# A two-layer hybrid backbone: four schedule numbers that hand out input products differently

## The chip, the cores and the metric

The kernel runs as one program on 1 core of one Trainium2 chip. The metric is device microseconds of that core. Three runs of the kernel before took 4359.16, 4373.27 and 4374.07 us; their median is 4373.27 us.

The engines are named as the profile names them: PE is TensorE's matmul, PEld its weight load, DVE is VectorE, ACT is ScalarE, POOL is GpSimd and SP is SyncE, which starts most DMAs here.

## The reference, cut to what matters

There are two layers over a trunk of 256 context tokens and 512 latent tokens. Layer 0 carries all 768 tokens, layer 1 only needs the 512 latent ones at its end. All tensors are fp32.

```python
def token_mixer(hc, hl, cos, sin, w_in, rw, cv, at, w_branch, w_out, ctx_out):
    zc = hc @ w_in                     # one input projection, 1024 -> 10112 columns
    zl = hl @ w_in
    ...
    o_rw_c, o_rw_l = rwkv_branch(rwc, rwl, *rw, ctx_out)      # bidirectional RWKV-7, 16 heads of 64
    o_at_c, o_at_l = attention_branch(atc, atl, *at, cos, sin, ctx_out)  # 8 q heads, 2 kv heads of 128
    o_cv_l = conv_branch(cvl, *cv)     # GLU, depthwise conv 31, LayerNorm, swish
    out_l = merge_branches(o_rw_l, o_cv_l, o_at_l, gtl, w_branch, w_out)
...
def merge_branches(o_rw, o_cv, o_at, z_gate, w_branch, w_out):
    branches = jnp.stack([o_rw, o_cv, o_at], axis=-2)
    proj = jnp.einsum('blnc,ncd->blnd', branches, w_branch)   # three 1024 x 1024 products
    gates = jax.nn.sigmoid(z_gate.reshape(proj.shape))
    return jnp.sum(gates * proj, axis=-2) @ w_out
```

After the mixer comes a norm, a residual and a squared-ReLU MLP (1024 -> 4096 -> 1024), again with norms.

## The kernel before, in words

**Products.** Each fp32 product is made of three fp32r products: `split` (L326) writes a high part on ACT and the rest on DVE or POOL, for the weights (`wh`, `wl`) and for the activations (`hh`, `hl`), and PE adds hi·hi, hi·lo and lo·hi. Products that are to be mixed into other work go into a queue: `job` (L392) appends 8 steps, one for each 128 rows of the weight, and `fill(n)` (L397) takes the next n steps off the queue and writes their matmuls (L412) into the program at that place. One step is called a *fill* here. In layer 0 it is six matmuls of 128x384 (768 tokens), in layer 1 three of 128x512. A fill whose step is 0 or 4 also asks for weights, two to four halves ahead: a DMA on SP (L372), the high part on ACT (L328) and the low part on DVE (L332).

**Spills.** The 36 column blocks of the input projection for attention and the gates (q 0 to 7, k and v 8 to 11, gates 12 to 35) are not used until after the RWKV part. `spill` (L1075) queues such a block, 8 fills, and its end (`spill_done`, L1081) copies the sum to a stage buffer on ACT and sends it to the DRAM tensor `z`.

**The pairs.** `rwkv_phase` (L1139) goes through 16 RWKV heads in 8 pairs. A pair has a merge and batch of small matmuls on PE, a serial chain between PE, DVE and ACT, and the readout; beside it runs the preparation of the next pair, ended by the solve. These are generators that yield estimated microseconds; `weave` (L1059) goes round them and calls `fill` for each estimated microsecond, in a ratio from `SCHED`. So the fills stand between the dependent steps of a pair. The queue also holds the pair's own input products and conv columns. Spills are queued at three places:

```python
            spills(F['early'])                                   # before pair 0
                cum = lambda p: round((32 - F['rest']) * p / 7)
                    spills(cum(p + 1) - cum(p))                  # in each of the pairs 0 to 6
                    spills(len(todo))                            # in the last pair: all that is left
```

After each solve, `s.fill(F['solve'])` takes up to 26 (layer 0) or 34 (layer 1) further fills of the queue. `rw_merge`'s first matmuls (L901) are kept behind the last fill.

**The load stage of attention.** What the last pair has not taken off the queue goes to `att_prep` (L556), which issues the loads of k, the rope table, q and v from `z` on SP (L481, L565) and prepares k and V. It calls `fill(len(s.jobs) // 3)` after each of two k heads and `fill(len(s.jobs) // 2)` after each of two v heads. `merge_phase` (L1250) then takes all that is left, closes the pool of `hh` and `hl`, opens the pool of `oh` and `ol` (9 buffers each) at its place, and makes the operands of branch 0 from the RWKV result (`of` loaded at L1273, `oh` on ACT, `ol` on POOL, both in `split`).

**The heads.** `att_head` (L594) runs 8 query heads, in layer 0 in two segments each (context and latent), in layer 1 in one. After each of its 128-query blocks it takes one fill, and at the end of each segment `pad` fills; these are products of branch 0, 64 fills in all.

**The conv norm.** After the heads, `merge_phase` steps through the LayerNorm of the conv branch with `for _ in range(ln): next(ln); s.fill(3)`: a product with `om` (L491), eight squares on ACT (L497) that POOL adds up in `csum` (L499), and the sum over channels (L502). Then it takes the remaining branch-0 fills and makes the operands of branch 2 from the attention result.

The framework's scheduler puts the instructions of each engine in an order of its own where the dependences allow it, by the program order and estimated costs.

Of the kernel before, what the change touches and what calls it, by code (L numbers as in the profile page):

```python
# [44 lines left out]

SCHED = [dict(open=1.3, first=0.55, mid=0.5, end=0.4, solve=26, early=4, tap0=1, tap1=1, merge=1.2, sums=0, grams=0, rest=9, ln=9, pad=1, last=1.15, tap2=1),
         dict(open=1.2, first=0.4, mid=0.4, end=0.4, solve=34, early=5, tap0=0.8, tap1=0.8, merge=1.4, sums=0, grams=0, rest=9, ln=9, pad=1, last=0.85, tap2=1.1)]


def shape_constants():
# [24 lines left out]
class Kern:  # L77
# [1061 lines left out]
    def rwkv_phase(s, l, P, T):  # L1139
# [3 lines left out]
        with ExitStack() as rc:  # L1143
# [18 lines left out]
            lat = T != TOK  # L1162
            F = s.sched = SCHED[l]
            s.tdebt, s.tratio = 0.0, F['tap0']
# [294 lines left out]
```

## Time and profile before

| | |
|---|---|
| median of 3 runs | 4373.27 us (4359.16 to 4374.07) |
| profiled execution | 4372.14 us |
| its span (first to last instruction) | 4370.4 us |
| mean granted TensorE clock | 0.963 |
| layer 0: merge of pair 1 to end of the last pair's chain | 367.9 to 1317.6 us |
| layer 0: load stage, heads, conv norm | 1317.6 to 1360.0, to 1574.2, to about 1596 us |
| layer 1: merge of pair 1 to end of the last pair's chain | 2611.9 to about 3570 us |
| layer 1: load stage, heads | to about 3607, to about 3782 us |

The stage borders are the starts of the first merge matmul of a pair (L901), of the rope product of k (L521), of the product with `om` (L491), and the end of the last step of the chain. The granted clock is given as a share of 2.4 GHz; 0.5 is 1.2 GHz.

### The profile page before, as it was taken

What the parts mean: (1) busy time and instruction counts of PE and PEld (TensorE: products, weight loads), DVE (VectorE), ACT (ScalarE), POOL (GpSimd) and SP (SyncE); (2) the same over time, 40 slices, a digit from 0 to 9 for tenths busy, and PEclk for the clock granted to TensorE, in tenths of its full rate; (3) what the DMA queues carried; (4) which work ended last, traced back from release to release, by engine and by line L of the source; (5) the groups of instructions that cost most, each with busy time, mean ns of one, the idle gap of its engine ahead of it and who ended that gap; (6) DMA issues with size and microseconds to landing.
All of it is one profiled execution on the core that took longest, in us unless ns stands there. A gap on an engine that the chain in (4) does not pass through costs nothing.

```text
span 4370.4 us, 77114 instructions
## 1 busy us (share of the span) xinstructions
PE 4141.8 (95%) x31232; PEld 3410.5 (78%) x31232; DVE 2723.4 (62%) x5238; ACT 1834.4 (42%) x3586; POOL 287.1 (7%) x349
## 2 busy tenths in 40 slices
PE   6999999999998989899999899999999989898998
PEld 4888888888886679689999677887777765575886
DVE  3788888888855554332323577888888855554344
ACT  3444445444534442332223445555545534433332
POOL 0000000000001022200000100000000000121001
PEclk9999999999999999899999889999999979998998
DMA  4212211112134234343322221112221232242332
GB/s 165 78 47 63 64 53 60 51 55 63 59 100 163 69 120 160 110 152 126 102 86 63 72 70 51 58 59 60 66 62 57 73 119 74 65 140 61 97 94 80
DMA packets 443595, 367.73 MB, mean 84 GB/s; under 512 B 19662, under 2 KB 391528, under 8 KB 437096
## 3 DMA queue, kind: packets, MB, share of 16 engines
q1 hardware_dynamic: 422504, 283.10, 21.6%
q10 hardware_dynamic: 20736, 79.70, 5.0%
q8 instruction: 247, 4.05, 0.4%
q14 instruction: 108, 0.88, 0.1%
HBM read 301.38 MB, written 53.48 MB: 81 GB/s over the span
## 4 chain that ended last, share of the span: by engine, by line
PE 80%; DVE 9%; ACT 5%; issue 2%; DMA 2%; POOL 2%; SPq 0%; ACTq 0%; DVEq 0%; POOLq 0%
PE mm L412 31%; PE mm L389 20%; PE g L815 3%; PE g L633 2%; PE g L939 2%; PE sp L960 2%; PE g L928 2%; PE S L612 2%; PE sp L964 1%; PE yp L978 1%; PE yp L976 1%; PE g L850 1%; PE g L1044 1%; PE g L824 1%; PE g L234 1%
## 5 line engine op out<-in xcount | busy, mean ns | idle before, releaser
L328 ACT ACTIVATE wh<-raw 128x512 fp32r<-128x512 f32 x700 | 441.4, 631 | 1249.8 <-PE mm L389 565.5
L332 DVE TENSOR_TENSOR wl<-raw,wh 128x512 fp32r<-128x512 f32 x700 | 502.0, 718 | 697.6 <-ACT wh L328 685.3
L412 PE MATMUL mm<-hh,wh 128*128 128x384 f32 (+1 forms) x2072 | 647.5, 371 | 15.3 <-ACT hh L328 4.8
L412 PE MATMUL mm<-hl,wh 128*128 128x384 f32 (+1 forms) x2072 | 637.9, 367 | 6.1 <-POOL hl L330 6.1
L412 PE MATMUL mm<-hh,wl 128*128 128x384 f32 (+1 forms) x2072 | 634.8, 365 | 0.0
L471 DVE SCALAR_TENSOR_TENSOR cv<-u,dw,cv 128x783 f32<-128x783 f32 (+1 forms) x480 | 426.7, 889 | 2.8
L412 PEld LDWEIGHTS mm<-hh,wh 128*128 128x128 f32 x2072 | 377.6, 192 | 55.1 <-ACT hh L328 7.3
L412 PEld LDWEIGHTS mm<-hl,wh 128*128 128x128 f32 x2072 | 382.6, 192 | 38.0 <-POOL hl L330 8.8
L412 PEld LDWEIGHTS mm<-hh,wl 128*128 128x128 f32 x2072 | 383.0, 192 | 30.5 <-issue 3.2
L412 PE MATMUL mm<-oh,wh 128*128 128x384 f32 (+1 forms) x768 | 252.9, 384 | 9.5 <-DVE acc L1285 6.0
L412 PE MATMUL mm<-ol,wh 128*128 128x384 f32 (+1 forms) x768 | 239.9, 365 | 10.2 <-POOL ol L330 10.2
L389 PE MATMUL mm<-hh,wh 128*128 128x384 f32 (+1 forms) x768 | 239.5, 367 | 5.3 <-ACT hh L347 3.6
L389 PE MATMUL mm<-hl,wh 128*128 128x384 f32 (+1 forms) x768 | 238.3, 365 | 5.1 <-POOL hl L330 4.6
L412 PE MATMUL mm<-oh,wl 128*128 128x384 f32 (+1 forms) x768 | 238.8, 364 | 0.0
L389 PE MATMUL mm<-hh,wl 128*128 128x384 f32 (+1 forms) x768 | 235.8, 362 | 0.0
L389 PE MATMUL mm<-fh,wh 128*128 128x384 f32 (+1 forms) x768 | 229.9, 353 | 0.0
L389 PE MATMUL mm<-fh,wl 128*128 128x384 f32 (+1 forms) x768 | 229.9, 353 | 0.0
L389 PE MATMUL mm<-fl,wh 128*128 128x384 f32 (+1 forms) x768 | 229.5, 352 | 0.0
L815 PEld LDWEIGHTS g<-KR,BK 64*128 64x128 f32 x1536 | 157.3, 204 | 43.0 <-issue 33.7
L815 PE MATMUL g<-KR,BK 64*128 64x128 f32 (+1 forms) x1536 | 178.3, 306 | 5.2 <-DVE KR L808 3.1
L412 PEld LDWEIGHTS mm<-oh,wh 128*128 128x128 f32 x768 | 139.6, 189 | 51.2 <-ACT wh L328 13.6
L966 ACT ACTIVATE S<-sp,lam 128x64 f32<-128x64 f32 x352 | 92.9, 310 | 206.3 <-PE sp L964 199.4
(297 smaller groups left out, 7239.0 us busy)
## 6 DMA issues: line engine op xcount, KB each, us to landing
raw<-in_w_in_dram SPq DMA_DIRECT2D x316, 256.0 KB
raw<-in_w_ff_dram SPq DMA_DIRECT2D x256, 256.0 KB
wmod<-in_w_mod_dram ACTq DMA_DIRECT2D x48, 1024.0 KB
raw<-in_w_branch_dram SPq DMA_DIRECT2D x96, 256.0 KB
z<-f ACTq DMA_DIRECT2D x40, 384.0 KB
gt<-z SPq DMA_DIRECT2D x24, 384.0 KB
raw<-in_w_out_dram SPq DMA_DIRECT2D x32, 256.0 KB
z<-f ACTq DMA_DIRECT2D x32, 256.0 KB
```

Source lines behind the costliest of these rows:

```text
L328: s.last_hi = nc.scalar.activation(out=hi, in_=src, func=AF.Copy)
L332: nc.vector.tensor_tensor(out=lo, in0=src, in1=hi.bitcast(F32), op=ALU.subtract)
L389: nc.tensor.matmul(ps[:, b, :t1 - t0], lhsT=w[:, k % 4, :], rhs=a[:, t0:t1], start=k == 0 and f == 0, stop=k == KT - 1 and f == 2)
L412: s.last_mm = nc.tensor.matmul(s.jps[:, b, :t1 - t0], lhsT=w[:, k % 4, :], rhs=a[:, t0:t1], start=k == 0 and f == 0, stop=k == KT - 1 and ...
L471: s.tap_pin(nc.vector.scalar_tensor_tensor(out=hold['c'], in0=u[:, k:k + L], scalar=w(k), in1=hold['c'], op0=ALU.mult, op1=ALU.add))
L612: nc.tensor.matmul(sps[:, b, :384], lhsT=lq, rhs=kT[kv][:, 384 * b:384 * b + 384], start=True, stop=True)
L633: nc.tensor.matmul(op[:, :nq], lhsT=V[:, kk, kv * 128:kv * 128 + 128], rhs=PT[:, kk, :nq], start=kk == 0, stop=kk == nk // 128 - 1)
L815: nc.tensor.matmul(gp[h][:, q, 0:n, :], lhsT=BK[ROWS[h], 4 * g + q].rearrange("p a b -> p (a b)"), rhs=KR[ROWS[h], 0:n, 4 * g + q, :], sta ...
L928: nc.tensor.matmul(wu[ROWS[h], q - q0], lhsT=TT[ROWS[h], q, :], rhs=KM[ROWS[h], q].rearrange("p a b -> p (a b)"), start=True, stop=True)
L939: nc.tensor.matmul(ap[ROWS[h], q - q0, 0:n, :], lhsT=W[ROWS[h], q, :], rhs=GB[ROWS[h], h, q, 0:n, :], start=True, stop=True)
L960: nc.tensor.matmul(sp[ROWS[h], d], lhsT=GB[d][:, h, q[d], 0, :], rhs=UV[d][:, h * 12 + q[d], :], start=d == 0, stop=d == 1 and k == 0)
L966: nc.scalar.activation(out=Sn[:, d], in_=sp[:, d], func=AF.Copy, scale=Q['lam', d][:, q[d]:q[d] + 1])
```

## The change: four numbers of the schedule tables

Two lines change, one for each layer. In layer 0 `rest` goes from 9 to 13 and `pad` from 1 to 0. In layer 1 `early` goes from 5 to 7 and `rest` from 9 to 14.

```diff
-SCHED = [dict(open=1.3, first=0.55, mid=0.5, end=0.4, solve=26, early=4, tap0=1, tap1=1, merge=1.2, sums=0, grams=0, rest=9, ln=9, pad=1, last=1.15, tap2=1),
-         dict(open=1.2, first=0.4, mid=0.4, end=0.4, solve=34, early=5, tap0=0.8, tap1=0.8, merge=1.4, sums=0, grams=0, rest=9, ln=9, pad=1, last=0.85, tap2=1.1)]
+SCHED = [dict(open=1.3, first=0.55, mid=0.5, end=0.4, solve=26, early=4, tap0=1, tap1=1, merge=1.2, sums=0, grams=0, rest=13, ln=9, pad=0, last=1.15, tap2=1),
+         dict(open=1.2, first=0.4, mid=0.4, end=0.4, solve=34, early=7, tap0=0.8, tap1=0.8, merge=1.4, sums=0, grams=0, rest=14, ln=9, pad=1, last=0.85, tap2=1.1)]
```

The number of all fills is the same. Where they are taken off the queue, counted in the program that the schedule writes (fills, before and after):

| place | layer 0 | layer 1 |
|---|---|---|
| weave of pair 0 | same | 21, 36 |
| weaves and solves of later pairs | 32 fewer | 39 fewer |
| weave of the last pair | 65, 65 | same |
| `att_prep`, after the k heads and v heads | 7, 39 | 17, 41 |
| each of the 8 heads | 8, 6 | same |
| conv norm, its first 9 steps | 0, 16 | 24, 24 |

The scheduler's order on PE follows this only roughly. Fill matmuls between the first merges of consecutive pairs, on PE, before and after (M1 is the first merge of pair 1):

| layer 0 | before | after | layer 1 | before | after |
|---|---|---|---|---|---|
| M1 to M2 | 432 | 425 | M0 to M1 | 264 | 381 |
| M2 to M3 | 384 | 402 | M1 to M2 | 360 | 317 |
| M3 to M4 | 393 | 385 | M2 to M3 | 254 | 267 |
| M4 to M5 | 453 | 384 | M3 to M4 | 295 | 259 |
| M5 to M6 | 354 | 372 | M4 to M5 | 256 | 235 |
| M6 to M7 | 438 | 355 | M5 to M6 | 264 | 223 |
| M7 to end of chain | 198 | 137 | M6 to M7 | 215 | 192 |
| end of chain to rope of k | 84 | 101 | end of chain to rope of k | 30 | 61 |
| rope of k to `om` | 419 | 497 | rope of k to `om` | 165 | 194 |
| `om` to L502 | 58 | 62 | before M0 | 24 fewer | |
| after L502 | 93 more | | | | |

PE's order in layer 0 around the rope product of k (`kraw`), where the load stage ends and head 0 begins (`vz` is raw v, `kT` the finished k, `qraw` a query head, L628 its transposes), before:

```order
L412 MATMUL mm<-hh,wh 128x384 x2
L412 MATMUL mm<-hl,wh 128x384 x2
L412 MATMUL mm<-hh,wl 128x384 x2
L521 MATMUL g<-kraw,rope 128x512 x2
L589 MATMUL g<-cst,vz 128x128 x4
L608 MATMUL S<-kT_13871,qraw 128x256
L589 MATMUL g<-cst,vz 128x128 x2
L608 MATMUL S<-kT_13871,qraw 128x256
L589 MATMUL g<-cst,vz 128x128 x6
L521 MATMUL g<-qraw,rope 128x512
L628 MATMUL g<-cst,Pm 128x128 x2
L612 MATMUL S<-kT_13871,qraw 128x384
```

The same place in the changed program:

```order
L412 MATMUL mm<-hh,wl 128x384
L521 MATMUL g<-kraw,rope 128x512
L412 MATMUL mm<-hh,wl 128x384
L412 MATMUL mm<-hh,wh 128x384 x2
L412 MATMUL mm<-hl,wh 128x384 x2
L412 MATMUL mm<-hh,wl 128x384 x2
L412 MATMUL mm<-hh,wh 128x384 x2
L412 MATMUL mm<-hl,wh 128x384 x2
L412 MATMUL mm<-hh,wl 128x384 x2
L412 MATMUL mm<-hh,wh 128x384 x2
L412 MATMUL mm<-hl,wh 128x384 x2
L412 MATMUL mm<-hh,wl 128x384 x2
```

Input products now stand between the two rope products of k; further blocks of them stand between the v transposes and the first query products. Before, none stood behind the first rope product.

SP's queue in layer 0 ahead of the loads of k and behind them (`bv` and `orw` belong to the last pair's readout, `raw` is a weight half), before:

```order
L475 DMA ocv<-cv 128x512
L372 DMA raw<-in_w_in_dram 128x4x128 x6
L372 DMA raw<-in_w_branch_dram 128x4x128 x2
L1005 DMA bv<-bv_d_89 128x768
L372 DMA raw<-in_w_branch_dram 128x4x128
L1027 DMA orw<-y 128x768
L372 DMA raw<-in_w_branch_dram 128x4x128
L481 DMA kraw<-z 128x768 x2
L565 DMA rope<-in_rope_dram 128x1152
L481 DMA qs<-z 128x768
L481 DMA vz<-z 128x768 x2
```

And in the changed program:

```order
L475 DMA ocv<-cv 128x512
L372 DMA raw<-in_w_in_dram 128x4x128 x6
L1005 DMA bv<-bv_d_89 128x768
L372 DMA raw<-in_w_in_dram 128x4x128
L1027 DMA orw<-y 128x768
L372 DMA raw<-in_w_in_dram 128x4x128
L481 DMA kraw<-z 128x768 x2
L565 DMA rope<-in_rope_dram 128x1152
L481 DMA qs<-z 128x768
L481 DMA vz<-z 128x768 x2
L481 DMA qs<-z 128x768 x7
L372 DMA raw<-in_w_in_dram 128x4x128 x2
```

Two weight halves fewer stand ahead of `kraw`, and the weights that follow the loads are those of input products.

POOL's queue in layer 0 from the heads to the conv norm (`ol<-of` up to L228 is branch 0 and the start of branch 2, later ones branch 2, `cvx` is branch 1), before:

```order
L330 TENSOR_TENSOR ol<-of,oh 128x768 x15
L228 MEMSET sc_16402 128x256
L229 COPY sc_16402<-sc 128x8x2
L499 TENSOR_TENSOR csum<-csum,csq 128x768
L330 TENSOR_TENSOR ol<-of,oh 128x768
L499 TENSOR_TENSOR csum<-csum,csq 128x768 x6
L330 TENSOR_TENSOR ol<-cvx,oh 128x768 x8
```

And in the changed program:

```order
L330 TENSOR_TENSOR ol<-of,oh 128x768 x9
L228 MEMSET sc_16402 128x256
L229 COPY sc_16402<-sc 128x8x2
L499 TENSOR_TENSOR csum<-csum,csq 128x768 x2
L330 TENSOR_TENSOR ol<-of,oh 128x768
L499 TENSOR_TENSOR csum<-csum,csq 128x768
L330 TENSOR_TENSOR ol<-of,oh 128x768
L499 TENSOR_TENSOR csum<-csum,csq 128x768 x4
L330 TENSOR_TENSOR ol<-of,oh 128x768 x5
L330 TENSOR_TENSOR ol<-cvx,oh 128x768 x8
```

Seven of branch 2's eight low parts now stand among the sums of the conv norm or behind them; before, seven of the eight stood ahead of them.

## Rows read from the trace of the kernel before

**Rows 1.** The page, part 1: busy time of each engine.

```profile
PE 4141.8 (95%) x31232; PEld 3410.5 (78%) x31232; DVE 2723.4 (62%) x5238; ACT 1834.4 (42%) x3586; POOL 287.1 (7%) x349
```

**Rows 2.** Windows: stretch, its us, busy us of each engine, clock, DMA share, GB/s.

```profile
1900.00:2400.00 500.00, 500.00 (x2902) 477.81 (x2900) 151.84 (x198) 126.32 (x185) 8.27 (x8) 1.00 0.31 98
1000.00:1140.00 140.00, 138.42 (x1406) 119.47 (x1403) 116.01 (x235) 65.36 (x140) 3.10 (x12) 1.00 0.20 61
2850.00:2960.00 110.00, 109.70 (x1096) 89.00 (x1095) 91.35 (x184) 57.07 (x126) 3.67 (x12) 1.00 0.22 65
```

**Rows 3.** Windows of L412 alone (PE, PEld, clock), layer 0, merge to merge.

```profile
512.90:651.10 138.20, 80.23 (x385) 65.09 (x384) 1.00 0.19 57
789.80:940.60 150.80, 93.44 (x453) 78.94 (x453) 0.99 0.18 56
940.60:1076.90 136.30, 76.83 (x354) 62.40 (x354) 0.97 0.20 59
1076.90:1225.10 148.20, 90.98 (x439) 74.63 (x438) 1.00 0.21 65
1225.10:1317.60 92.50, 46.59 (x198) 35.50 (x198) 0.94 0.31 100
```

**Rows 4.** Timeline of PE, layer 0, last fills and the rope of k.

```profile
1335.75 0.51 PE L412 MATMUL mm<-hh,wh 128*128 128x384 f32 x2
1336.10 0.51 PE L412 MATMUL mm<-hl,wh 128*128 128x384 f32 x2
1336.44 0.51 PE L412 MATMUL mm<-hh,wl 128*128 128x384 f32 x2
1343.37 1.19 PE L521 MATMUL g<-kraw,rope 128*128 128x512 f32 x1 [6.41 <-DMA vz<-z]
```

**Rows 5.** Windows of all instructions, layer 0, rope of k to head 0's products.

```profile
1343.40:1360.00 16.60, 14.17 (x43) 7.51 (x43) 9.68 (x22) 8.05 (x17) 0.32 (x1) 0.81 0.83 321
1344.00:1347.00 3.00, 3.00 (x8) 1.23 (x7) 1.75 (x4) 0.94 (x1) 0.00 (x0) 0.62 1.03 413
```

**Rows 6.** Windows of all instructions, layer 0, the heads.

```profile
1360.00:1574.20 214.20, 206.67 (x924) 144.29 (x922) 114.81 (x234) 105.51 (x220) 27.47 (x17) 1.00 0.28 88
```

**Rows 7.** Timeline of POOL, layer 0, the first operands and the conv norm.

```profile
1359.68 3.60 POOL L330 TENSOR_TENSOR ol<-of,oh 128x768 fp32r<-128x768 f32 x2 [200.88 <-DMA oat<-os]
1583.03 12.60 POOL L499 TENSOR_TENSOR csum<-csum,csq 128x768 f32<-128x768 f32 x6
```

**Rows 8.** Timeline of PE, layer 0, the sum over channels.

```profile
1595.68 2.08 PE L502 MATMUL g<-csum,ones 128*1 128x384 f32 x3 [6.71 <-POOL csum L499]
```

**Rows 9.** Windows of L412 alone, layer 1, merge to merge.

```profile
2611.90:2743.10 131.20, 69.08 (x265) 48.57 (x264) 0.93 0.18 52
2743.10:2876.50 133.40, 79.77 (x361) 61.88 (x360) 1.00 0.21 62
2876.50:2995.40 118.90, 63.74 (x255) 44.50 (x254) 1.00 0.20 61
3257.20:3380.20 123.00, 66.09 (x264) 46.91 (x264) 1.00 0.21 63
```

**Rows 10.** Timeline of PE, layer 1, last fills and the rope of k.

```profile
3583.28 0.39 PE L412 MATMUL mm<-hl,wh 128*128 128x512 f32 x1
3583.51 0.40 PE L412 MATMUL mm<-hh,wl 128*128 128x512 f32 x1
3592.92 2.04 PE L521 MATMUL g<-kraw,rope 128*128 128x512 f32 x2 [9.01 <-DMA qs<-z]
```

**Rows 11.** Windows of all instructions, layer 1, rope of k to head 0's products.

```profile
3592.90:3606.80 13.90, 9.81 (x23) 4.89 (x23) 6.82 (x9) 4.55 (x8) 2.93 (x2) 0.62 0.87 315
```

## The prediction, as it went on record

> **What bounds the kernel now.** I read the busy times first. PE is busy 95% of the span and no other engine over 62% [rows 1], so the question is whether the products that move cost the same wherever they stand. The windows come next. In the MLP PE has no gap; in the pairs it is busy too, 138.42 of 140 us and 109.70 of 110, at full clock, with DVE at 83% in both [rows 2]. A fill matmul that stands in a pair may fill a gap that a serial step leaves, or may lengthen the pair. The same pass over stretches that hold the same work and a different number of fills tells which [rows 3, 9]. Last come the two load stages, where the timeline shows PE idle: 6.41 us before the rope of k in layer 0 and 9.01 us in layer 1 [rows 4, 10], both put down to DMAs, and behind each a stretch at reduced clock with gaps [rows 5, 11].
>
> **The change, part by part.** The numbers of fills are unchanged, so everything rests on the price of a matmul in the place it leaves against the place it goes to. Price at full clock with nothing in the way: four 128x384 matmuls in 1336.44 − 1335.75 = 0.69 us, so 0.173 each; one 128x512 in 0.23 [rows 4, 10].
>
> *Layer 0, the pairs: 131 fill matmuls fewer between the merges of pairs 1 and 7, 61 fewer in the last pair's chain.* Price in a pair from the slopes: 453 matmuls in 150.8 us against 354 in 136.3 is 14.5/99 = 0.146; 439 in 148.2 against 385 in 138.2 is 10.0/54 = 0.185 [rows 3]. I take 0.16: −131 x 0.16 = −21, and −61 x 0.16 = −10 in the last pair. Where fewer products leave PE gaps the clock may fall: the last stretch, with 198 products in 92.5 us, has 0.94, the one with 354 has 0.97 [rows 3]. For more of this I put +3. Together −28; ends −33 (0.173 each, no clock loss) and −15 (half price).
>
> *Layer 0, the load stage: 191 matmuls more between chain end and `om`, apart from the pads.* At 0.173 that is +33. Some of it is hidden. Of the idle 6.41 us before the rope of k [rows 4], the 17 matmuls more ahead of it take 3, and about 2 more come because two weight halves fewer are queued on SP ahead of `kraw` and so the loads start earlier: 5. Between the rope of k and head 0, PE is busy 14.17 of 16.6 us at clock 0.81 [rows 5], which is 14.17 x 0.81 = 11.5 us at full clock; products that fill the 2.4 us of gaps and keep the clock up could save 16.6 − 11.5 = 5.1. So +33 − 10 = +23. Ends: +31 if the loads, whose share of DMA is 0.83 there, delay the new products' weights by as much as they hide, and +13 if as much again is hidden in head 0.
>
> *Layer 0, the pads.* The heads lose 16 fills, 96 matmuls. In the heads PE is busy 206.67 of 214.2 us [rows 6]; the gaps may grow, so I take 0.14 a matmul, under 0.173: −97 x 0.14 = −13. The 93 matmuls after L502 come back at full price, as that part has no gap to fill: +16. In front of L502, 58 become 62, so the wait of 6.71 us for POOL's seven sums [rows 7, 8] stays. Behind it comes a new wait: five low parts of branch 2 stand behind the sums on POOL, 1.80 us each (3.60 for two [rows 7]), and branch 2's products need one every 6 x 0.173 = 1.04 us: 5 x 0.76 = 4. Two others go between the sums, 3.6 us, partly in front of L502's wait. PE has kept branch-0 products to cover some. I take +5. Sum +8; ends −1 (the heads give full price, −17, and POOL is covered) and +16 (no cover of the 3.6 and the 4, heads at 0.10).
>
> *Layer 0 together: −28 + 23 + 8 = +3.*
>
> *Layer 1, before and in the pairs.* 24 matmuls leave before the first merge of pair 0: −3.6 at 0.15. From there to the merge of pair 1 there are 381 instead of 264. That stretch took 131.2 us at clock 0.93, a later one with the same 264 took 123.0 at 1.00 [rows 9]; with 117 more at 0.13 on a clock that no longer falls, 123 + 15 = 138, which is +7. The later stretches lose 43, 36, 21, 41, 23 and gain 13: 151 fewer. Slopes here are (133.4 − 118.9)/(361 − 255) = 0.137 and (133.4 − 123.0)/(361 − 264) = 0.107 [rows 9]; at 0.12, −18. Clock falls where products go below 255: +5. Sum −10; ends −18 and 0.
>
> *Layer 1, the load stage: 60 matmuls more from chain end to `om`.* At 0.23 that is +14. Of the 9.01 us wait [rows 10], 31 matmuls take 31 x 0.23 = 7.1. The stretch behind it is busy 9.81 of 13.9 us at clock 0.62 [rows 11], 6.1 us of work at full clock, so 29 matmuls find room for 6.7: hidden about 13. But the region of `hh` and `hl` is freed later, so the operands of branch 0, and with them head 0's fills, come later: +2. So +3; ends 0 and +10. *Layer 1 together: −7.*
>
> **Sum.** +3 − 7 = −4. The profiled execution of before took 4372.14 us (span 4370.4 and 1.7 outside it), so 4368. It stands 1 us under the median of the runs, 4373.27, so no correction is made between them.
>
> **The rivals.** Half a per cent is 22 us and about what a measurement can tell from no change: below 4351 is faster, above 4395 slower.
>
> *A: the load stages swallow what they are given.* For it: two waits on DMA and two stretches at clocks 0.81 and 0.62, and one of 3.00 us at 0.62 with the DMA share at 1.03 [rows 5], so nothing waits there for PE. Against it: there are 191 and 60 matmuls to hide, 33 and 14 us, and the gaps add up to about 10 and 13. If the clock loses nothing in the pairs (−31 in layer 0, −15 in layer 1), the load stages cost +13 and 0, and the pads +1 (heads −17, behind L502 +16, POOL +2), the sum is −32: about 4340.
>
> *B: the kept products become the thing that head 0 waits for.* The pool of `oh` and `ol` lies where `hh` and `hl` are, so the eight operand splits of branch 0 cannot start before the last kept product; PE's queue then holds 48-matmul blocks between the k ropes, the v transposes and head 0's first products, while ACT and DVE, which make k and V, wait behind them. For it: the order on PE, and POOL's first low part, which begins at 1359.68 already now, 200.88 us after its last work, right where head 0 begins [rows 7]. Against it: PE works meanwhile, so only idle time counts. If nothing of layer 0's 33 us hides, the operands add 8 idle us (four splits at 1.8), and the pads are −13 + 16 + 7 = +10 with POOL's new wait uncovered, layer 0 is −28 + 33 + 8 + 10 = +23; with layer 1's pairs at −6 and its load stage at +10 the sum is +27: 4399. It decides from the point where nothing is hidden and PE's waits for `ol` pass 10 us.
>
> *C: PE in the pairs has slack that its busy time hides.* PE's busy time in the pairs may be modelled over gaps: PEld is busy 477.81 of 500 us in the MLP (96%), but 119.47 of 140 (85%) and 89.00 of 110 (81%) in the pairs [rows 2]. If products there were all in gaps, removing them would give nothing: pairs 0, load stages +31 and +6, pads 0: about 4409. The slopes of rows 3 and 9, 0.107 to 0.185 a matmul, speak against it. The Trainium skill (page "Perfetto Trace Analysis", section "Identifying the Most-Contended Engine") says that matmul busy time is no good measure and that weight-load busy time is one; by it the pairs have 15 to 19% of slack, and the trace bears the slack out but not that the products cost nothing.
>
> *D: the change moves little, since the scheduler keeps its own order.* The counts show that it doesn't: 192 of the 2652 fill matmuls between the merge of pair 1 and the end of the last chain are elsewhere. It would give 4372, inside the forecast.
>
> **How the numbers follow.** Chances: forecast, with D, 0.64 (its own range 4352 to 4390); A 0.21; B 0.12; C 0.03. So faster by over 0.5% 0.21, within 0.64, slower 0.15. The ends of the unknown costs are −17 to +16 of layer 0's pads and load stage and ±10 of layer 1; added as independent they give about ±20, and reaching to A and near B, 4338 to 4396.
>
> **What the changed profile would show.** Right: stretches between merges of pairs 4 and 7 of layer 0 near 140, 139 and 135 us, and layer 1's first pair near 138; the idle before the rope of k nearly gone in both layers; clock near 1.0 from there to head 0; chain end to `om` of layer 0 longer by 10 us (23 − 13), and five low parts on POOL behind `csum` with a wait of `ol` on PE. Wrong: pair stretches that stay as long with fewer products (C), a load stage of layer 0 no longer than before (A), or PE idle more than 10 us for `oh` or `ol` in head 0 (B).

## The result and the profile after

The changed kernel took 4413.59 us (median of 4 runs, 4402.1 to 4433.16) against 4372.16 for the kernel before (4 runs, 4359.16 to 4374.07). The ratio of the executions is 1.0106, 95% interval 1.0062 to 1.0150 (that of the two medians is 1.0095): slower by 1%, where 4368 was forecast, and outside the range. One execution of the kernel before, taken beside the later runs, lasted 5647.74 us at a mean granted clock of 0.643, and no ratio counts it.

The span of the profiled execution is 4418.5 us, 48.1 more than before. Its busy times are those of [rows 1] within 1.4%:

```profile
PE 4173.6 (94%) x31232; PEld 3455.2 (78%) x31232; DVE 2709.7 (61%) x5238; ACT 1835.7 (42%) x3586; POOL 286.8 (6%) x349
```

The same number of matmuls, 31232, keeps PE busy 32 us longer, and the mean granted clock is 0.950 instead of 0.963. To find the place, windows of all instructions from the merge of pair 1 (layer 0) and of pair 0 (layer 1) to the end of the chain; first the kernel before:

```profile
367.90:1317.50 949.60, 939.50 (x9734) 814.62 (x9734) 763.49 (x1518) 443.94 (x958) 19.26 (x72) 0.99 0.21 63
2611.90:3570.10 958.20, 939.74 (x9525) 750.87 (x9524) 770.73 (x1644) 483.18 (x1061) 27.34 (x84) 0.95 0.21 61
```

and the same two stretches of the changed kernel:

```profile
368.50:1315.80 947.30, 930.07 (x9543) 807.54 (x9542) 752.73 (x1510) 434.70 (x946) 18.23 (x72) 0.95 0.19 59
2623.80:3617.60 993.80, 949.12 (x9486) 762.12 (x9488) 769.72 (x1641) 480.07 (x1053) 28.72 (x84) 0.92 0.19 57
```

Layer 0's pairs have 191 matmuls fewer and are only 2.3 us shorter; the clock fell from 0.99 to 0.95. Layer 1's have 39 matmuls fewer and are 35.6 us longer, at 0.92 instead of 0.95. Windows of L412 alone, which answer to [rows 3], and of layer 1, which answer to [rows 9]:

```profile
795.60:939.70 144.10, 83.00 (x384) 68.03 (x384) 0.95 0.17 53
939.70:1084.30 144.60, 82.14 (x372) 67.31 (x372) 0.95 0.18 54
1084.30:1223.80 139.50, 78.19 (x355) 63.97 (x355) 0.94 0.20 64
1223.80:1315.80 92.00, 36.34 (x137) 26.34 (x137) 0.81 0.27 83
```

```profile
2623.80:2782.60 158.80, 90.05 (x381) 68.28 (x381) 0.90 0.17 52
2911.80:3045.60 133.80, 70.61 (x267) 49.73 (x267) 0.91 0.19 55
3312.30:3431.10 118.80, 53.98 (x223) 39.17 (x223) 1.00 0.19 56
```

In the last line 223 products go through at full clock in 118.8 us; in the line above it 267 need 133.8 at 0.91. Summed over the whole span, the record of the granted clock holds 443.4 us at 1.2 GHz after and 327.6 before: 115.8 more. "Half-clock time" below is this record's sum over a stretch; twice (1 − clock) times the stretch's length gives it roughly.

The waits of the load stages came out as thought. PE in layer 0 around the rope of k, which answers to [rows 4]:

```profile
1339.99 1.10 PE L521 MATMUL g<-kraw,rope 128*128 128x512 f32 x2 [0.99 <-DVE kT L581]
1340.53 0.74 PE L412 MATMUL mm<-hh,wl 128*128 128x384 f32 x1
```

The wait of 6.41 us is now 0.99, and in layer 1 that of 9.01 us [rows 10] is 1.50. The windows behind them, which answer to [rows 5, 11], are at full clock:

```profile
1340.00:1357.00 17.00, 17.00 (x95) 15.76 (x96) 6.96 (x13) 6.07 (x11) 0.00 (x0) 1.00 0.93 343
3640.40:3654.30 13.90, 11.18 (x47) 7.63 (x47) 6.26 (x9) 6.35 (x12) 1.46 (x2) 1.00 0.92 325
```

One wait was foreseen neither by the forecast nor by a rival. PE in layer 1, between the merges of pairs 0 and 1; first the kernel before, then the changed one:

```profile
2673.48 1.12 PE L882 MATMUL g<-key,cst 128*128 128x512 f32 x2 [1.30 <-DVE key L876]
```

```profile
2713.13 2.05 PE L882 MATMUL g<-key,cst 128*128 128x512 f32 x2 [11.78 <-DVE key L876]
```

PE stands still for 11.78 us, instead of 1.30, before the bonus product of pair 1 (L882), whose key DVE had not got to.

**Where the 48.1 us are**, stage by stage of the two profiled executions (length after minus before, half-clock time after minus before):

| stretch | us | half-clock us |
|---|---|---|
| start to merge 1 | +0.7 | +3.4 |
| layer 0, merge 1 to end of chain | −2.4 | +64.8 |
| layer 0, end of chain to `om` | −1.9 | −10.2 |
| layer 0, `om` to the end of the three branches' products (scaling of `acc`, L1330) | +15.2 | +3.4 |
| from there to merge 0 of layer 1 | +0.2 | +3.4 |
| layer 1, merge 0 to merge 1 | +27.6 | +13.7 |
| layer 1, merge 1 to end of chain | +8.1 | +60.6 |
| layer 1, end of chain to the end | +0.5 | −23.3 |

### The profile page after: what moved, and what is told of

It is laid out like the page before. It is cut to its first block, busy times and chain, and to the rows that moved or that the text cites. A ratio compares the mean times of both kernels' runs of the same rounds, so it can differ in the third digit from the quotient of the medians.

```text
span 4418.5 us, 77108 instructions
## 1 busy us (share of the span) xinstructions
PE 4173.6 (94%) x31232; PEld 3455.2 (78%) x31232; DVE 2709.7 (61%) x5238; ACT 1835.7 (42%) x3586; POOL 286.8 (6%) x349
## 5 line engine op out<-in xcount | busy, mean ns | idle before, releaser
L412 PE MATMUL mm<-hh,wh 128*128 128x384 f32 (+1 forms) x2072 | 654.1, 375 | 24.9 <-ACT cv L453 9.6
L412 PE MATMUL mm<-hl,wh 128*128 128x384 f32 (+1 forms) x2072 | 647.6, 370 | 6.2 <-POOL hl L330 6.2
L412 PE MATMUL mm<-hh,wl 128*128 128x384 f32 (+1 forms) x2072 | 650.8, 371 | 1.1 <-DVE wl L332 1.0
L412 PEld LDWEIGHTS mm<-hh,wh 128*128 128x128 f32 x2072 | 386.5, 195 | 66.5 <-ACT cv L453 10.3
L412 PEld LDWEIGHTS mm<-hl,wh 128*128 128x128 f32 x2072 | 389.7, 195 | 38.5 <-POOL hl L330 8.8
L412 PEld LDWEIGHTS mm<-hh,wl 128*128 128x128 f32 x2072 | 391.4, 196 | 34.3 <-DVE wl L332 2.4
L412 PE MATMUL mm<-oh,wh 128*128 128x384 f32 (+1 forms) x768 | 249.4, 378 | 2.2 <-DVE acc L1285 0.8
L412 PE MATMUL mm<-ol,wh 128*128 128x384 f32 (+1 forms) x768 | 240.3, 366 | 8.3 <-POOL ol L330 8.2
L389 PE MATMUL mm<-hl,wh 128*128 128x384 f32 (+1 forms) x768 | 238.4, 365 | 5.1 <-POOL hl L330 4.6
L412 PE MATMUL mm<-oh,wl 128*128 128x384 f32 (+1 forms) x768 | 237.4, 363 | 0.0
L389 PE MATMUL mm<-hh,wl 128*128 128x384 f32 (+1 forms) x768 | 236.2, 362 | 0.0
L389 PEld LDWEIGHTS mm<-hh,wh 128*128 128x128 f32 x768 | 142.3, 192 | 36.6 <-ACT wh L328 15.9
```

Source lines behind the costliest of these rows:

```text
L389: nc.tensor.matmul(ps[:, b, :t1 - t0], lhsT=w[:, k % 4, :], rhs=a[:, t0:t1], start=k == 0 and f == 0, stop=k == KT - 1 and f == 2)
L412: s.last_mm = nc.tensor.matmul(s.jps[:, b, :t1 - t0], lhsT=w[:, k % 4, :], rhs=a[:, t0:t1], start=k == 0 and f == 0, stop=k == KT - 1 and ...
```

## The experiments

Three theories. *Clock*: a product keeps its price, but where pairs have too few the clock falls, and takes back what their going gave. *Slack* (rival C): products in pairs stand in gaps and cost nothing; the lower clock is a symptom. *Late inputs*: in layer 1, `early` 7 puts pair 1's k and r behind 16 more fills. Each ratio is to the kernel before, run on the same chip.

**1. Layer 0's half alone.**

```diff
-grams=0, rest=9, ln=9, pad=1, last=1.15
+grams=0, rest=13, ln=9, pad=0, last=1.15
```

> Layer 0's half of the change alone (rest 13, pad 0; layer 1 as before). Clock theory: a fill matmul keeps its price of 0.16 to 0.17 us at full clock, but TensorE's clock falls where the pairs have fewer of them, and what the products give back the clock takes: half-clock time between the merge of pair 1 and the end of the chain rises from 20 to about 85 us, the stretch stays within 5 us of before's 949.6, and the sum is +10 to +16 (about 4385), made behind the conv norm. Slack theory (rival C: products in pairs stand in gaps and cost nothing): the same stretch, but then its length minus half of the half-clock time must not fall either. If the loss were layer 1's alone: within 5 us of before.

4378.94 us, ratio 1.0023 (1.0007 to 1.0039); profiled span 4378.7. The sum is +8.5 in the medians, a little under the expected +10, and the loss stands behind the conv norm as expected: `om` to the scaling of `acc` is 15.2 us longer. Merge 1 to end of chain took 942.8 us with 75 at half clock, 6.8 less than before, where a change of at most 5 was expected. The test set for the slack theory goes against it: the length minus half of the half-clock time falls from 939.4 to 905.2. What matters more is a comparison that this run gave for nothing. Its layer 0 is the same program as that of the changed kernel. The stretch from merge 6 to merge 7, in the changed kernel:

```profile
1084.30:1223.80 139.50, 136.96 (x1393) 119.31 (x1393) 116.89 (x240) 61.97 (x138) 3.08 (x12) 0.94 0.20 64
```

and in this one:

```profile
1088.90:1221.20 132.30, 129.81 (x1391) 112.52 (x1391) 116.78 (x239) 61.89 (x138) 3.01 (x12) 1.00 0.21 68
```

Same instructions, same busy DVE and ACT, and 7.1 us between them (by the unrounded borders) that go with the clock alone: 16.8 us of half clock against none, 0.42 us lost for each. That the lower clock is only a symptom is refuted by this pair of rows, since the program is the same in both. In the three other traces with these layer-0 pairs (runs 4, 6 and 8) the stretch has 0, 10.1 and 16.9 us at half clock and takes 132.4, 136.6 and 139.6 us. The ten executions of this run say the same of the whole: the quickest has a span of 4366.3 us at a mean clock of 0.962, the longest 4392.9 at 0.955.

**2. `early` alone; 3. `rest` of layer 1 alone.**

```diff
-early=5, ... rest=9
+early=7, ... rest=9        (run 2)
+early=5, ... rest=14       (run 3)
```

> One number of layer 1 alone: early 7 instead of 5. Late-inputs theory: 16 more fills stand ahead of pair 1's k and r in the queue, so its preparation starts after pair 0's chain is through, PE idles about 12 us ahead of the bonus product (L882) and then runs at half clock: merge 0 to merge 1 takes 155 to 160 us instead of 131. Later pairs and the last one have fewer products: the rest within 10 us. Sum +10 to +25. Rival (the price of the products alone): 117 matmuls at 0.13 are +15 without an idle PE, merge 0 to merge 1 near 146, sum within 5 us.

> One number of layer 1 alone: rest 14 instead of 9. Clock theory: pairs 1 to 6 have some 100 matmuls fewer, 12 us at 0.12, and 40 to 60 us more half-clock time, so they are 5 to 15 us longer; load stage and heads +10 for 105 more products of which some hide; sum +10 to +20. Slack theory: the pairs keep their length, +5 to +10. Forecast's prices: pairs -12, sum near 0.

Run 2: 4400.8 us, 1.0072 (1.0049 to 1.0096), some 30 us over the kernel before and above the expected band. Merge 0 to merge 1 took 158.9 us, as expected, and the idle PE is there with the same length:

```profile
2695.72 2.04 PE L882 MATMUL g<-key,cst 128*128 128x512 f32 x2 [11.78 <-DVE key L876]
```

Behind merge 1 the pairs are 10.5 us longer to the end of the chain, for 63 products fewer and with 39 us more at half clock, just outside the 10 that were expected.

Run 3: 4384.98 us, 1.0043 (1.0025 to 1.0061), inside the expected band. Merge 1 to merge 7 is 4.2 us longer for 101 products fewer, with 44 us more at half clock: the clock's loss as expected, the length just under the expected 5 to 15. `kraw` to `om` is 12.8 longer for 72 more products. Both parts of layer 1 lose, `early` more.

**4. Layer 0's `rest` without its `pad`.**

```diff
-grams=0, rest=9, ln=9, pad=1, last=1.15
+grams=0, rest=13, ln=9, pad=1, last=1.15
```

> Layer 0's rest 13 without its pad 0 (pad stays 1; layer 1 as before). The pairs as in the run of layer 0 alone, the heads 97 matmuls more (+10 to +13), nothing moved behind the conv norm (-15 to -18 there): 4375 to 4385, 3 to 8 us under the run of layer 0 alone. If the pads were neutral: the same as the run of layer 0 alone.

4394.28 us, 1.0061 (1.0046 to 1.0076): 9 us above the expected band and 15 above run 1, where 3 to 8 below run 1 was expected, so the sign was wrong. The profiled execution, with a span of 4384.6, is its quickest, 5.9 above run 1's. From the rope of k to `om`, this run and then run 1, with pad 0 and otherwise the same:

```profile
1333.90:1587.00 253.10, 246.63 (x1139) 181.52 (x1140) 126.10 (x263) 121.61 (x248) 27.83 (x17) 1.00 0.35 112
```

```profile
1338.10:1568.90 230.80, 225.11 (x1042) 165.22 (x1042) 119.05 (x257) 114.44 (x238) 16.84 (x11) 1.00 0.33 107
```

22.3 us for 97 matmuls, 0.23 each; with pad 0, behind `om`, they cost 14.2 us. So by its stages pad 0 gains some 8 us in this setting.

**5. Products that nothing reads, in layer 1's last pair.** Between its merge and the end of its chain the kernel before has 30 products and 39 us at half clock. Added to the kernel before, 8 or 4 after each of ten sums of squares:

```diff
             nc.vector.tensor_copy(rs[:, 0, j, o // 128:], cps[:, o // 128:])
+            if T != TOK:
+                s.dummy(8)          # the other run: 4
             yield 1.4
...
+    def dummy(s, n):
+        ps = s.g([128, 512])
+        for k in range(n):
+            s.nc.tensor.matmul(ps, lhsT=s.hh[:, k % 8, CTX:CTX + 128], rhs=s.hh[:, (k + 1) % 8, CTX:TOK], start=k == 0, stop=k == n - 1)
```

> The kernel before with 80 products that nothing reads, 8 after each of the ten sums of squares (L544 before) in the last pair of layer 1, whose 41 us at half clock hold almost no product. Clock theory: the clock of that stretch rises, half-clock time from 39 to under 15 us, which at 0.4 us per us (the same program's stretch of pair 6, 132.4 against 139.5 us with 0 and 16.8 us at half clock) gives back 10 us; the products cost 80 x 0.12 to 0.23 = 10 to 18: merge 7 to chain end 68 to 77 us, sum 0 to +8. Slack theory (the clock costs nothing there and products are hidden): the stretch stays at 68. Products without any gain of the clock: 78 to 87 us.

> The same with 40 products, 4 after each sum. Clock theory: if they are enough to raise the clock, 39 to about 15 us at half clock, -10, and +5 to +9 for the products: 63 to 68 us and sum -5 to 0; if not, half-clock time stays and the stretch is 73 to 77 us. Slack theory: 68.

4374.19 us, 1.0004 (0.9994 to 1.0013), and 4371.9 us, 1.0001 (0.9992 to 1.0011). The stretch before, with 4 and with 8 (windows of all instructions):

```profile
3501.80:3570.10 68.30, 67.80 (x804) 56.21 (x804) 31.87 (x79) 24.42 (x64) 0.00 (x0) 0.71 0.22 64
```

```profile
3511.40:3578.50 67.10, 66.20 (x838) 52.60 (x840) 31.95 (x79) 24.37 (x64) 0.00 (x0) 0.90 0.22 65
```

```profile
3506.10:3578.40 72.30, 71.98 (x878) 57.93 (x880) 32.30 (x79) 24.30 (x64) 0.00 (x0) 0.95 0.20 61
```

Forty products of no use make the stretch 1.2 us *shorter*: the clock goes from 0.71 to 0.90. At 0.42 us for each of the 25.7 us of half clock saved, 10.8 come back, so the forty cost 9.6, 0.24 each. Eighty cost 4.0 + 0.42 x 32.5 = 17.7, 0.22 each. So products raise the clock, and pay for themselves with it about once. Both stretches lie in the expected bands. The length alone does not decide between the theories, since 67.1 is also near the slack theory's 68: the 0.42 comes from run 1. That the clock costs time in this stretch too, the same program shows: in the kernel before and runs 1, 4 and 7 the stretch has 36.2 to 40.4 us at half clock and takes 67.2 to 69.1 us, the longest with the most.

**6. The same in the changed kernel's layer 1**, 35 in each of the pairs 1 to 6, from `weave` as estimated microseconds go by.

```diff
                     s.pe(us)
+                    s.dn += us * s.dr       # s.dr is 0.6 in pairs 1 to 6 of layer 1, else 0; set elsewhere
+                    if s.dn >= 2:
+                        s.dummy(int(s.dn))
+                        s.dn -= int(s.dn)
```

> The changed kernel with 35 products that nothing reads in each of the pairs 1 to 6 of layer 1, 210 in all, spread over their weaves. Clock theory: half-clock time between merge 1 and merge 7 falls from 99 to under 50 us and gives back some 20 us, the products cost 210 x 0.12 = 25: the stretch stays near 768 us and the kernel near 4414, with a higher mean clock: products pay for themselves. Theory of the products alone (clock lost through something else): the clock stays and the time rises by 25.

4438.52 us, 1.0152 (1.0136 to 1.0167). Merge 1 to merge 7: half-clock time fell from 98.9 to 51.2 us as expected, but the stretch rose by 12.7 us and the kernel by 25. At 0.42 the clock gave back 20, so 210 products less 15 fills that moved out cost 33, 0.17 each: more than the 0.12 expected. Here they do not pay for themselves. The kernel's +25 is the figure of the theory of the products alone, but what that theory rests on, an unchanged clock, did not come. This run's layer 0 is again the changed kernel's program, and its last pair repeats the comparison of run 1; the changed kernel's, then this one's:

```profile
1223.80:1315.80 92.00, 91.45 (x1003) 79.96 (x1003) 39.70 (x83) 32.50 (x76) 0.00 (x0) 0.81 0.27 83
```

```profile
1224.70:1307.30 82.60, 81.51 (x1001) 70.31 (x1003) 39.68 (x83) 32.49 (x76) 0.00 (x0) 0.94 0.29 93
```

9.4 us for 23.9 us of half clock, 0.39 each.

**7. `pad` 0 alone.**

```diff
-grams=0, rest=9, ln=9, pad=1, last=1.15
+grams=0, rest=9, ln=9, pad=0, last=1.15
```

> One number of layer 0 alone: pad 0 instead of 1. From the runs with pad 1 and pad 0 at rest 13: the heads -22 (97 matmuls, 0.23 each), behind the conv norm's sum +15: -7, about 4363. If the gain in the heads was bound to the fuller load stage: heads -13 to -17, sum 0. The forecast's +8 for this part would make 4380.

4368.6 us, 0.9990 (0.9977 to 1.0003): it can't be told from the kernel before. By stages the rope of k to `om` is 21.9 us shorter and `om` to the scaling of `acc` 16.3 longer, near the −22 and +15 that were expected, though the kernel's time is 6 us above the expected 4363. The forecast's +8 for this part is outside the interval.

**8. The two extra blocks behind pair 1's inputs.** The changed kernel, with only the order of the queue changed in layer 1:

```diff
-            spills(F['early'])
+            spills(min(F['early'], 5))
...
             s.rw_inputs(l, P, 1, T, In, 'kr')
+            spills(F['early'] - 5 if l else 0)
```

> The changed kernel with layer 1's two extra early blocks queued behind pair 1's k and r instead of ahead of them; the same products in all. Late-inputs theory: the 11.8 us in which PE waits ahead of the bonus product (L882) go, and the half-clock time behind them with them: merge 0 to merge 1 145 to 150 us for 357 products instead of 158.8 for 381, of which 24 products stand ahead of merge 0 again (+4); the kernel 5 to 12 us faster than the changed one. Theory that the number of products there makes the stretch long: about 155, no gain.

4402.11 us, 1.0066 (1.0049 to 1.0083), 11.5 us under the changed kernel's median, as expected, though the two intervals overlap; the stage shows it more clearly. Merge 0 to merge 1, in the changed kernel and in this one:

```profile
2623.80:2782.60 158.80, 145.34 (x1351) 120.07 (x1351) 111.68 (x220) 68.64 (x145) 3.41 (x12) 0.90 0.17 52
```

```profile
2628.40:2763.60 135.20, 135.07 (x1328) 110.73 (x1327) 107.70 (x218) 69.58 (x146) 2.32 (x12) 1.00 0.22 64
```

The wait before L882 is gone, PE has no gap, the clock never falls, and 23 matmuls fewer take 23.6 us less, more than the late-inputs theory had expected. 24 products at 0.13 are 3 of it; the rest is the wait and the clock behind it. With these 3 added back, the stretch takes the 138 us that the prediction gave it.

**9. The other directions: `rest` 5 in both layers, `early` 4, and fewer fills in a block behind each solve of layer 1.**

```diff
-rest=9                      (both layers)
+rest=5
-early=5                     (layer 1)
+early=4
-first=0.4, ... solve=34     (layer 1)
+first=0.5, ... solve=22
```

> The other direction: rest 5 in both layers, so the pairs take four blocks more than before and the load stages start with an empty queue. Clock theory: the pairs of layer 0 are at full clock already, so 180 more products cost 0.16 each, +29, and the last pair and load stage, with 54 and 84 fewer, give back less, since the load stage waits for its DMAs anyway (-9 -8, and the clock falls there); layer 1 has 30 to 40 products more in pairs, 10 us less at half clock: sum +5 to +15. If clock were all: -10 in layer 1 and 0 in layer 0, faster than before.

> Layer 1's early 4 instead of 5, the other direction of early 7. Late-inputs theory: pair 1's k and r come 8 fills sooner; before, PE had one wait of 3.1 us and 17 us at half clock in that stretch, so merge 0 to merge 1 takes 120 to 126 us instead of 131.3; one block more goes to the load stage and the later pairs: sum -5 to +3. If only the number of products counts: 254 instead of 264 products, 130 us.

> Layer 1 with solve 22 instead of 34 and first 0.5 instead of 0.4: fewer fills in a block behind each solve, more spread between the pair's steps. Clock theory: half-clock time between merge 1 and merge 7, 34 us before, falls to 10 to 20 and the stretch of 758 us by 5 to 10, if where the products stand counts and not only how many; sum -5 to -10. If only their number counts: the same time as before within 3 us.

`rest` 5: 4411.58 us, 1.0091 (1.0076 to 1.0106), far outside what was expected. Layer 0's empty load stage did as expected, at clock 0.57:

```profile
1331.60:1355.30 23.70, 7.71 (x30) 4.73 (x27) 10.79 (x24) 4.04 (x10) 0.00 (x0) 0.57 0.34 118
```

But layer 1's pairs took 988.1 us instead of 958.2, with 42 us more at half clock and 30 products *more*. Of these 30 us the clock, at 0.39 to 0.42, is some 17; the rest is not explained. `early` 4: 4378.04 us, 1.0011 (1.0001 to 1.0020), some 6 above the kernel before, where at most +3 was expected. Merge 0 to merge 1 took 125.4 us, inside the expected band, but this shows little: the unchanged program took 125.6 us there in run 7 and 127.0 in run 1, against the 131.3 of the kernel before's trace. `solve` 22: 4397.22 us, 1.0058 (1.0038 to 1.0078), against an expected gain; merge 0 to end of chain 995.6 us at clock 0.92.

So in layer 1 the number of products in a pair does not set its clock. Counted from the traces, fill matmuls in slices of 10 us from a merge of layer 1 on (a star: over 3 us of it at half clock):

```
before,  merge 4    21 13 8 7 13 13 2* 4* 17 15 51 54 38 21
after,   merge 4    9* 21* 8 10 0 0* 5* 12* 17 18 29 53 43 17
after,   merge 5    17 5 7 0 0 20 8 23 14 55 43 33
rest 5,  merge 3    16 44* 3 11 10 12 8 4* 8* 18 13 43 54 26
```

The end of each pair holds 30 to 55, which is PE at work on little else, and the clock falls at the start or in the middle, mostly where fills have been few (the slice of 44 in `rest` 5 is an exception). Adding products, or taking them out of the last block, did not help there. Nor do fills alone tell it: the pair from merge 5 has two slices without any and keeps its clock; what the pair's own products did there was not counted. Which order would keep the clock up was not found.

**The traces side by side.** Many of these traces hold the same program in a stretch, so the price of the clock can be tried on them. From each length 0.39 us is taken off for each us at half clock; the 0.39 is that of run 6's last pair, which lies in none of these stretches.

| merge 1 to merge 7 | traces | fill matmuls | us | half-clock us | us less 0.39 of it |
|---|---|---|---|---|---|
| layer 0, `rest` 5 | 1 | 2580 | 870.8 | 0.0 | 870.8 |
| layer 0, `rest` 9 | 8 | 2454 | 854.6 to 858.5 | 6.8 to 13.7 | 851.8 to 853.3 |
| layer 0, `rest` 13 | 5 | 2323 | 850.7 to 860.7 | 41.0 to 64.9 | 834.7 to 835.7 |
| layer 1, as before | 6 | 1644 | 758.6 to 767.7 | 34.1 to 58.0 | 744.2 to 746.1 |
| layer 1, changed | 2 | 1493 | 765.1, 767.5 | 95.6, 99.0 | 727.9, 728.9 |

Lengths of one program that differ by up to 10 us come within 2 us of each other. What is left between the programs is the price of the products: 0.13 to 0.14 us each in layer 0, 0.11 in layer 1. So both are real, products cost time and the clock takes it back. In layer 0 the time at half clock also grows step by step as products go; whether by their number or by their new order, these runs do not separate. Layer 1 with `rest` 5 and with `solve` 22 has 755.7 and 755.1 by the same sum, for 1650 and 1624 products: 10 us there come from neither.

## Why the prediction was wrong

**The step that failed** is the clock in the pairs: "For more of this I put +3" in layer 0 and "Clock falls where products go below 255: +5" in layer 1. At the 0.4 us per us measured in runs 1 and 6, the 64.8 us more at half clock in layer 0 are +26 and the 60.6 us behind merge 1 of layer 1 +24. A second step failed beside it, layer 1's first pair (below). Against the forecast's terms these three stretches came out 26, 21 and 21 us longer; in layer 0 the stretch from chain end to `om` and the one behind `om` came out 12 and 6 us shorter, which hid a part of it. Two rows showed the fall [rows 3, 0.94 and 0.97], and one row its price [rows 9, 131.2 against 123.0]; they were taken as a small correction to products that go, when it is a price of its own on all that is left in the stretch.

The Trainium skill (page "TensorE: Matmul & The Clock Gate", section Terms) puts the penalty of a throttled clock at the throttled time times (1 − K/N), where K/N is the granted share: half of it here. The runs have 0.39 to 0.42 where DVE and ACT have part of the work. By the rule the 115.8 us more at half clock are 58 us; by the measured price 45 to 49; the span grew by 48.1. That these two agree is partly luck, since the 48.1 also hold the 11.78 us of idle PE and what the moved products gave and cost.

**Layer 0's pairs, the price of a product.** Right. Without the clock's +26, −2.4 is −28; the forecast had −31 before its clock term. The slopes of rows 3 stood between stretches at nearly full clock, and so gave the price at full clock only.

**Layer 0's load stage, +23.** Right: run 4 has −1.5 + 22.2 = +20.7 for it. **The pads, +8.** Wrong in sign by the stages, −8 in run 4 against run 1 and −5.6 in run 7: the heads gave 0.23 a matmul, not 0.14. Why a product costs that much there was not tried. Behind `om` +15.2, where +21 was expected. The wait before L502 did not stay at 6.71 us [rows 8]:

```profile
1592.38 2.72 PE L502 MATMUL g<-csum,ones 128*1 128x384 f32 x4 [9.59 <-POOL csum L499]
```

POOL now has two `ol` between its sums. The five behind them were covered: PE waited 0.9 us for `ol` in all from `om` to the scaling of `acc`.

**Layer 1's first pair, +7.** Wrong by 21: the stretch took 27.6 more. The step priced the 117 products rightly, as run 8 shows, and forgot what they were queued in front of. The clue stood in the change: the fills of a queue come in order, and pair 1's k and r were in it. **Layer 1's load stage, +3.** Right: chain end to `om` +0.9.

**The rivals.** C gave the nearest time, 4409, for a wrong reason: it took the products to be free, and the sums over all traces give 0.11 to 0.14 us for each; its number was luck. B's wait of head 0 did not come: the first low part of branch 0 starts at 1377.87 instead of 1359.68 [rows 7], and PE stays busy, 208.16 of 213.6 us:

```profile
1357.00:1570.60 213.60, 208.16 (x950) 149.56 (x949) 111.89 (x244) 108.23 (x228) 16.86 (x11) 1.00 0.29 90
```

A's condition, a clock that loses nothing in the pairs, was not met; with the clock's part taken out, layer 0's pairs are −27 or −28, near A's −31.

Some of the size stays open. Runs of one kernel differ by 10 to 30 us, and stretches of the same program differ by whether they fall to half clock, so run 1's 8 us and runs 2 and 3's 30 and 15, 53 together, do not add up to the 41 of the whole change in a strict sense. Why the clock falls where it does in layer 1 stays open. No version beat the kernel before beyond its interval.

## What to carry to other kernels

Before taking filler work out of a latency-bound stretch, look at what granted clock that stretch and its neighbours have: the filler's price is not only its own time but also what the slower clock does to all the work left behind, and in layer 0's pairs the two were about equal here, so moving it gained nothing. In layer 0 fewer products went with a lower clock; in layer 1 the total of products in a stretch did not tell its clock; the windows' clock column did. And when a FIFO queue gets more entries, name what stands behind them: the next stage's inputs may be in it.

## What the runs showed of the hardware

The same instructions on the same data ran in 139.5 or 132.3 us, and in 92.0 or 82.6, by the granted clock alone, which differed between traces that hold the same instructions there. Over five traces of the same layer-0 pairs the stretch from merge 1 to merge 7 took 850.7 to 860.7 us, 0.39 us more for each us at half clock. Forty 128x512 products whose result nothing reads, added to a stretch of 68.3 us, left it at 67.1 and raised its clock from 0.71 to 0.90.
